# Splitting the prompt's q and k into high and low parts where they are projected, and scoring two attention heads in row tiles of TensorE

## The chip, the core and the metric

The kernel runs on one core of a Trainium2 chip. The core has five engines that run programs of their own and wait for each other on semaphores: TensorE (PE, matmuls, with its weight loads shown as PEld), VectorE (DVE), ScalarE (ACT), GpSimd (POOL) and SyncE (SP, which here only issues DMAs). The metric is the device time of one execution in microseconds (us); lower is better.

## The reference, cut to what matters

One step of a decoder layer for a prompt of 2048 tokens and 32 sample tokens (8 requests of 4), width 1024, all in float32. Half of the mixing width is a gated linear recurrence (HGRN), the other half is attention in 8 heads of 64 channels. Only the prompt's attention is touched by the change:

```python
proj = a @ w_in                                  # a = rmsnorm(x), q, k, v of attention are the last 3*512 columns
q_b = partial_rotary(qb, pos); k_b = partial_rotary(kb, pos)
for window, dil in ((128, 1), (512, 4), (2048, 16)):     # DILATIONS
    # positions of one residue mod dil form a sub-sequence; a query sees the last window/dil + 1 of its own
    s = where(valid, q*scale @ k, NEG_INF)               # blocks of 128 queries
    m = s.max(-1); p = exp(s - m); l = p.sum(-1); acc = p @ v
o_b = sum_d(exp(m_d - max m) * acc_d) / sum_d(exp(m_d - max m) * l_d)
h = x + concat(o_a, o_b) @ w_o;  h = h + ConvFFN(rmsnorm(h));  h = h + gate * (p @ w_ple_proj);  y = rmsnorm(h)
```

The kernel joins two of the dilations in one set of blocks with an additive mask, so the code has two kinds of blocks, `di` 0 and 1.

## The kernel before

The program has three parts in time. First **the projection** (`in_phase`, twice 1024 tokens, up to about 827 us): `x @ w_in` with each factor cut into a rounded high part and a low part, three matmuls for a product (L301, L302, L303). Its token groups go to q, k, v and so on; for a group of 128 prompt tokens `late()` turns q or k on TensorE (L324), copies it out of PSUM with one VectorE copy (L329, tile `oT`), and SP stores it to a scratch tensor in DRAM (L330, `qT_d`, `kT_d`). HGRN units run in the side. Then **the attention phase** (`attn_phase`, about 827 to 1208 us), and last the output projection, ConvFFN and embedding, two thirds of the time, which the change leaves alone.

In the attention phase the 8 heads are taken as 4 pairs `p`; a pair has 32 blocks of 128 queries: 16 with `di` 0 (the queries of one residue mod 4 in a chunk `c` of 512 tokens; it sees `nk` = c+1 groups of 128 keys) and 16 with `di` 1 (`nk` 2, the first one 1). For each block a pipeline of three steps runs over the turns of one loop:

- `scores`: matmuls into a PSUM tile S (one bank, two buffers), then for each head a VectorE reduction that adds the mask and takes the minimum (L724, into `st`) and a ScalarE exponential (L725). Signs are arranged so that the minimum serves as maximum. A block with `nk` 1 or 2 is one `Unit` for both heads; one with `nk` 3 or 4 is two `Unit`s, one a head.
- `turned`, two turns later: TensorE transposes P into a PSUM tile PT (L732), and one copy takes it to SBUF (L734, on ScalarE in every fourth turn, else on VectorE).
- `weighted`, three turns later: the product with v (L744) into `acc`, the two heads in the two column halves of TensorE; after four blocks ScalarE copies it out (L802).

Score precision: q is kept as high over low on 128 partitions (`qS`: 64 channels high, 64 low), k as `kH` and `kL`, both repeated on the two halves, so that two matmuls of K=128 make all four products. To build these, `stage` issues four SP DMAs for a chunk (L600, each half of the partitions twice), and `stack` runs on POOL two roundings (L142), two subtractions for the low half of q (L611) and two for `kL` (L616), on VectorE two casts into the residue order `q4` (L612), on ScalarE two casts `kH` (L615). There are 4 x 4 chunks.

`merge` joins the two kinds of blocks for a chunk: small VectorE and ScalarE work on the statistics, a store of coefficients to DRAM (L672), a load that spreads them over the partitions (L676, tile `cf`, two buffers), and two POOL multiplications (L681).

One turn in two, a step of the side work is put between: HGRN unit 7, then the sample tokens' attention (32 loads of 1 MB of cached keys and values, matmuls L844 and L880), then the samples' HGRN (L567, L570, L584). The framework's scheduler sets the final order on each engine by its own costs; each engine then runs its list in order.

## Time and profile before

| | |
|---|---|
| median of 3 runs | 3099.36 us (3092.71 to 3101.87) |
| the profiled execution | 3096.28 us, its span 3094.5 us |
| PE, DVE, ACT, POOL busy | 97%, 72%, 42%, 26% of the span |
| attention phase, 827 to 1208 us | 381 us, 12% of the span |
| PE, DVE, ACT, POOL busy in it | 339.5, 301.5, 241.0, 162.2 us |

A busy PE is not a PE at its peak: matmuls are pipelined and their ends are modelled, so that the distance between starts says what a matmul costs, and its own duration does not. Rows of groups give the line, the engine, the operation, the tiles, the count, the busy time and mean nanoseconds, and behind the bar the idle time of the engine ahead of it with what ended it. A row of the answer on windows gives, for a stretch, its length, then the busy time of PE, PEld, DVE, ACT and POOL (with counts), the granted clock of TensorE as a share of full speed, the share in which the 16 DMA engines were busy, and the GB/s they moved.

### The profile page before, as it was taken

What the parts mean: (1) busy time and instruction counts of PE and PEld (TensorE: products, weight loads), DVE (VectorE), ACT (ScalarE), POOL (GpSimd) and SP (SyncE); (2) the same over time, 40 slices, a digit from 0 to 9 for tenths busy, and PEclk for the clock granted to TensorE, in tenths of its full rate; (3) what the DMA queues carried; (4) which work ended last, traced back from release to release, by engine and by line L of the source; (5) the groups of instructions that cost most, each with busy time, mean ns of one, the idle gap of its engine ahead of it and who ended that gap; (6) DMA issues with size and microseconds to landing.
All of it is one profiled execution on the core that took longest, in us unless ns stands there. A gap on an engine that the chain in (4) does not pass through costs nothing.

```text
span 3094.5 us, 52057 instructions
## 1 busy us (share of the span) xinstructions
PE 2992.3 (97%) x19035; PEld 2785.2 (90%) x19035; DVE 2233.4 (72%) x4662; ACT 1295.2 (42%) x2813; POOL 806.6 (26%) x659
## 2 busy tenths in 40 slices
PE   9999999999889989999999999999999999999997
PEld 8988899987675667998999998999998999999997
DVE  7424667867587686568777779777789877777776
ACT  4111422222276564335444444444445444445443
POOL 1111122222343342002222232222222222222331
PEclk9999999999999999999999999999999999999998
DMA  5234333342539976673443445333434444436443
GB/s 185 93 121 135 105 104 104 106 141 81 158 79 284 285 225 218 237 265 139 137 133 113 133 156 168 124 126 131 144 119 162 153 139 139 144 116 219 132 166 130
DMA packets 265216, 467.97 MB, mean 151 GB/s; under 512 B 39360, under 2 KB 107072, under 8 KB 263168
## 3 DMA queue, kind: packets, MB, share of 16 engines
q1 hardware_dynamic: 261376, 397.66, 40.7%
q10 hardware_dynamic: 3584, 66.98, 6.1%
q8 instruction: 150, 2.46, 0.3%
q14 instruction: 106, 0.87, 0.1%
HBM read 381.05 MB, written 150.48 MB: 172 GB/s over the span
## 4 chain that ended last, share of the span: by engine, by line
PE 80%; DVE 12%; DMA 3%; issue 2%; ACT 1%; POOL 1%; SPq 0%; DVEq 0%; ACTq 0%; POOLq 0%
PE mm L136 18%; PE mm L137 18%; PE mm L138 18%; PE mm L301 3%; PE mm L302 3%; PE mm L303 3%; PE acc L744 1%; PE lv L441 1%; PE PT L732 1%; DVE w L910 1%; DVE P L724 1%; PE lv L301 1%; PE lv L303 1%; PE lv L302 1%; PE S L719 1%
## 5 line engine op out<-in xcount | busy, mean ns | idle before, releaser
L137 PE MATMUL mm<-w 128*128 128x352 f32 (+3 forms) x3768 | 1212.4, 322 | 4.3 <-DVE w L982 4.3
L138 PE MATMUL mm<-w 128*128 128x352 f32 (+3 forms) x3640 | 1164.0, 322 | 0.0
L136 PE MATMUL mm<-w 128*128 128x352 f32 (+3 forms) x3640 | 1138.7, 323 | 18.2 <-ACT w L981 8.7
L137 PEld LDWEIGHTS mm<-w 128*128 128x128 f32 x3768 | 712.9, 189 | 8.0 <-DVE w L982 7.8
L136 PEld LDWEIGHTS mm<-w 128*128 128x128 f32 x3640 | 681.8, 189 | 24.6 <-ACT w L981 10.6
L910 DVE TENSOR_TENSOR w<-raw,w 128x512 fp32r<-128x512 f32 x718 | 563.1, 799 | 179.5 <-ACT w L909 172.7
L138 PEld LDWEIGHTS mm<-w 128*128 128x128 f32 x3640 | 687.7, 189 | 0.1
L909 ACT CAST w<-raw 128x512 fp32r<-128x512 f32 x718 | 431.9, 620 | 396.3 <-PE mm L138 277.2
L1171 DVE TENSOR_TENSOR h<-h,mm 128x352 f32<-128x352 f32 (+1 forms) x528 | 257.6, 506 | 83.8 <-PE mm L138 83.2
L1103 POOL TENSOR_TENSOR raw<-raw 128x512 f32<-128x512 f32 x66 | 97.2, 1473 | 725.2 <-DMA raw<-in_w_gate_dram 251.0
L1111 POOL TENSOR_TENSOR raw<-raw 128x512 f32<-128x512 f32 x66 | 93.4, 1414 | 384.8 <-DVE w L910 384.8
L725 ACT ACTIVATE P<-P,st 128x256 f32<-128x256 f32 (+3 forms) x256 | 134.3, 527 | 75.5 <-DVE st L724 68.4
L1126 ACT COPY s<-mm 128x352 f32<-128x352 f32 (+1 forms) x198 | 88.2, 445 | 173.7 <-PE mm L138 169.2
L301 PE MATMUL mm<-wh,xh 128*128 128x512 f32 x352 | 142.0, 405 | 0.0
L303 PE MATMUL mm<-wh,xl 128*128 128x512 f32 x352 | 140.9, 401 | 0.0
L302 PE MATMUL mm<-wl,xh 128*128 128x512 f32 x352 | 140.4, 400 | 0.0
L142 POOL TENSOR_SCALAR wh<-wraw 128x512 fp32r<-128x512 f32 x96 | 72.0, 762 | 245.5 <-PE o L137 82.5
L136 PE MATMUL mm<-xh,wh 128*128 128x384 f32 (+2 forms) x384 | 124.9, 330 | 5.6 <-ACT xh L199 4.9
L724 DVE CUSTOM_DVE_ANT_0 P<-S,mask 128x256 f32<-128x256 f32 (+3 forms) x256 | 105.6, 445 | 29.7 <-PE S L720 25.3
L963 POOL TENSOR_TENSOR w<-w 128x704 f32<-128x704 f32 (+2 forms) x42 | 75.1, 1794 | 198.9 <-ACT w L962 198.2
L224 DVE TENSOR_TENSOR wl<-wraw,wh 128x512 fp32r<-128x512 f32 x104 | 84.6, 835 | 58.2 <-POOL wh L142 52.1
L138 PE MATMUL mm<-xh,wl 128*128 128x384 f32 (+2 forms) x384 | 125.1, 329 | 1.3 <-DVE wl L224 1.2
(337 smaller groups left out, 5156.3 us busy)
## 6 DMA issues: line engine op xcount, KB each, us to landing
raw<-in_w_gate_dram SPq DMA_DIRECT2D x132, 256.0 KB
raw<-in_w_up_dram SPq DMA_DIRECT2D x132, 256.0 KB
raw<-in_w_down_dram SPq DMA_DIRECT2D x132, 256.0 KB
out_sk_dram<-in_cache_k_dram ACTq DMA_DIRECT2D x56, 584.0 KB
out_sv_dram<-in_cache_v_dram ACTq DMA_DIRECT2D x56, 584.0 KB
wraw<-in_w_in_dram SPq DMA_DIRECT2D x104, 256.0 KB
raw<-in_w_ple_gate_dram SPq DMA_DIRECT2D x64, 256.0 KB
raw<-in_w_o_dram SPq DMA_DIRECT2D x48, 256.0 KB
```

What stands on the lines that cost most here:

```text
L136: PE.matmul(ps, lhsT=wh, rhs=xh, start=first, stop=False, skip_group_check=read)
L137: PE.matmul(ps, lhsT=wh, rhs=xl, start=False, stop=False, skip_group_check=read)
L138: PE.matmul(ps, lhsT=wl, rhs=xh, start=False, stop=last, skip_group_check=read)
L301: PE.matmul(ps, lhsT=xh[k][:, js], rhs=wh, start=k == 0, stop=False)
L302: PE.matmul(ps, lhsT=xh[k][:, js], rhs=wl, start=False, stop=False)
L303: PE.matmul(ps, lhsT=xl[k][:, js], rhs=wh, start=False, stop=k == NK - 1)
L724: V.tensor_tensor_reduce(pe, s[:, w * i:w * i + w], bl.mask, 1.0, 3e38, ALU.add, ALU.min, mn)
L725: A.activation(pe, pe, AF.Exp, bias=mn, scale=-1.0, accum_out=st[:, bl.r, hh, 0:1])
L909: A.copy(w[:, 0], raw)
L910: V.tensor_sub(w[:, 1], raw, f32(w[:, 0]))
L1103: G.tensor_add(s1, a21, a22)
L1171: V.tensor_add(h[m][:, cs], h[m][:, cs], ps[:, :H])
```

## The change

`late()` now makes both parts itself: a ScalarE copy rounds the turned q or k to the high part (for k in the residue order within 128 tokens), a VectorE subtraction makes the low part, and SP stores both; 64 stores in all where there were 32. The scratch tensors have a dimension for high and low. In the attention phase `fetch` loads a chunk of q and of k, both parts at once, with two DMAs on POOL's own queue (a software queue, which the kernel did not use so far), and `stack` is left with two POOL roundings that put q into `q4`. Gone are the SP loads of `stage`, the subtractions L611 and L616 and the casts L612 and L615.

A score is three products, high by high, high by low, low by high, each of K=64; the two heads of a pair sit in the upper and lower 64 partitions and go to the two row tiles of TensorE, so three pairs of matmuls stand where two heads had two matmuls each. S is one tile of two banks (`S = pS.tile([128, 2, 512])`, made once), one for each head; blocks with one or two key groups use its halves in turn. A block is one `Unit` for both heads; where `nk` is 3 or 4 it has two PT tiles, one copied by VectorE and one by ScalarE, and takes two turns of the side work. Lines of the second kernel are a few higher: scores L727, transposes L743, products L753, `cf` multiplications L683, roundings L144, loads L618.

```diff
@@ in_phase, late()
-                            oT = ev.tile([128, 4, 128], F32, name="oT", bufs=2)
-                            V.tensor_copy(oT, ptv)
-                            SP.dma_start((qT_d if kind == "q" else kT_d)[:, :, tok:tok + 128], oT)
+                            oT = [ev.tile([128, 4, 128], F32R, name="oT", bufs=3) for _ in range(2)]
+                            hi, lo, pv = *oT, ptv
+                            if kind == "k":
+                                hi, lo = [t.rearrange("p a (r i) -> p a r i", r=4) for t in (hi, lo)]
+                                pv = ptv.rearrange("p a (i r) -> p a r i", r=4)
+                            A.copy(hi, pv)
+                            V.tensor_sub(lo, pv, f32(hi))
+                            for i in range(2):
+                                SP.dma_start(f32((qT_d if kind == "q" else kT_d)[:, i, :, tok:tok + 128]), f32(oT[i]))
@@ attn_phase
...
+        def fetch(p, c):
+            cs = slice(512 * c, 512 * c + 512)
+            for i, (t, src) in enumerate(((q, qT_d), (k, kT_d))):
+                if p or c:
+                    G.dma_start(t[:, :, cs], src[:, :, p, cs])
+                else:
+                    A.copy(t[:, 0, cs], first[i][:, 0])
+                    round_g(t[:, 1, cs], first[i][:, 1])
+        def stack(c):
+            for x in range(2):
+                round_g(q4[:, x, :, 128 * c:128 * c + 128],
+                        f32(q[:, x, 512 * c:512 * c + 512]).rearrange("p (i r) -> p r i", r=4))
@@ Unit.scores
-                s = pS.tile([128, 512], F32, name="S")
-                for i, hh in enumerate(self.heads):
-                    PE.matmul(s[:, w * i:w * i + w], lhsT=bl.q(hh), rhs=bl.k(kH, hh), start=True, stop=False)
-                    PE.matmul(s[:, w * i:w * i + w], lhsT=bl.q(hh), rhs=bl.k(kL, hh), start=False, stop=True)
+                s = S[:, :, self.at:self.at + w]
+                for i, (a, b) in enumerate(((0, 0), (0, 1), (1, 0))):
+                    for hh in range(2):
+                        PE.matmul(s[:, hh], lhsT=bl.q(hh, a), rhs=bl.k(hh, b), start=i == 0, stop=i == 2,
+                                  tile_position=(64 * hh, 0))
@@ Unit.turned
-                (A.copy if on_act else V.tensor_copy)(out[:, :n], pt[:, :n])
+                for i, heads in enumerate(((0,), (1,)) if nk > 2 else ((0, 1),)):
...
+                    act = i if nk > 2 else on_act
+                    (A.copy if act else V.tensor_copy)(self.pt[:, heads[0]:heads[-1] + 1], pv)
@@ when chunks are loaded and prepared, in blocks ahead of their use
-                    x = begin[p, 0, 0] - 10 + 4 * c
-                    at(x - 7, lambda p=p, c=c: staged.append(stage(p, c)))
-                    at(x, lambda p=p, c=c: stack(c, *staged.pop(0)))
+                        x = begin[p, 0, 0] - 6 + 4 * c
+                    at(x - 6, lambda p=p, c=c: fetch(p, c))
+                    at(x - 2, lambda c=c: stack(c))
```

**TensorE, two blocks of `di` 1.** In the rows below S is the score tile, PT the transposed P, acc the product with v, and 128x256 is the size written. Before, a block of two heads:

```order
L719 MATMUL S<-kH,qS 128x256 [waits DVE_49]
L720 MATMUL S<-kL,qS 128x256
L719 MATMUL S<-kH,qS 128x256
L720 MATMUL S<-kL,qS 128x256
L732 MATMUL PT<-c_ident,P 128x128 [waits DVE_49,Activation_49]
L732 MATMUL PT<-c_ident,P 128x128 [waits Activation_49]
L744 MATMUL acc<-pt,v 64x128
L744 MATMUL acc<-pt,v 64x128 [waits Activation_49]
L744 MATMUL acc<-pt,v 64x128 x6
```

And in the changed kernel, such a block (p 3):

```order
L727 MATMUL S<-k,q 128x256 [waits DVE_49]
L727 MATMUL S<-k,q 128x256 x5
L743 MATMUL PT<-c_ident,P 128x128 [waits Activation_49]
L743 MATMUL PT<-c_ident,P 128x128
L743 MATMUL PT<-c_ident,P 128x128 [waits Activation_49]
L743 MATMUL PT<-c_ident,P 128x128
L753 MATMUL acc<-pt,v 64x128 [waits DVE_49]
L753 MATMUL acc<-pt,v 64x128 x3
```

Four matmuls became six. The wait on VectorE ahead of the first of them was, before, for the minimum of the S tile two back (in 145 of 166 cases); now it is for that of the block right ahead (126 of 127), since both halves belong to one tile S. The side work stands earlier against the blocks: HGRN unit 7 ended near block 34 and now near block 16, the samples' attention ran over blocks 40 to 106 and now 21 to 76, the samples' HGRN over 113 to 127 and now 79 to 94.

**POOL at the start of the attention phase.** ssq and rb are the two tiles in which the first chunk was loaded. Before:

```order
L142 TENSOR_SCALAR qS<-ssq 128x512 [waits PE_49]
L142 TENSOR_SCALAR qS<-ssq 128x512
L611 TENSOR_TENSOR qS<-ssq,qS 64x512 [waits Pool_49]
L616 TENSOR_TENSOR kL<-rb,kH 128x4x128 [waits PE_49,Activation_49,Pool_49]
L611 TENSOR_TENSOR qS<-ssq,qS 64x512 [waits Pool_49]
L616 TENSOR_TENSOR kL<-rb,kH 128x4x128 [waits Activation_49,Pool_49]
L142 TENSOR_SCALAR qS<-stage 128x512 [waits DMAHW7_49,DMAHW0_49]
L142 TENSOR_SCALAR qS<-stage 128x512
```

Now (q_8221 is `q4`; the waits of the second load are for stores into `kT_d`):

```order
L144 TENSOR_SCALAR q<-ssq 128x512 [waits PE_49]
L144 TENSOR_SCALAR k<-rb 128x512
L618 DMA k<-kT_d 128x2x512
L618 DMA k<-kT_d 128x2x512 [waits DMAHW3_49,DMAHW5_49,DMAHW2_49,DMAHW7_49,DMAHW1_49,DMAHW0_49]
L144 TENSOR_SCALAR q_8221<-q 128x4x128 [waits PE_49,Pool_49]
L144 TENSOR_SCALAR q_8221<-q 128x4x128 [waits Activation_49]
L618 DMA q<-qT_d 128x2x512 [waits Pool_49]
```

The six POOL operations that made the first chunk are four, with two loads between them.

**POOL between the first and the second pair of heads.** o_ are the accumulated outputs. Before:

```order
L616 TENSOR_TENSOR kL<-stage,kH 128x4x128 [waits DMAHW6_49,DMAHW5_49,Activation_49]
L616 TENSOR_TENSOR kL<-stage,kH 128x4x128 [waits Activation_49]
L611 TENSOR_TENSOR qS<-stage,qS 64x512 [waits Pool_49]
L611 TENSOR_TENSOR qS<-stage,qS 64x512
L681 TENSOR_TENSOR o_8398<-o_8398,cf 128x512 [waits DMAHW5_49,DMAHW4_49,Pool_49]
L681 TENSOR_TENSOR o_9168<-o_9168,cf 128x512
L826 MEMSET qb 128x1024 [waits DVE_49]
L681 TENSOR_TENSOR o_8570<-o_8570,cf 128x512 [waits DMAHW6_49,DMAHW5_49]
L681 TENSOR_TENSOR o_9305<-o_9305,cf 128x512
```

Now:

```order
L683 TENSOR_TENSOR o_8464<-o_8464,cf 128x512 [waits DMAHW1_49,DMAHW0_49]
L683 TENSOR_TENSOR o_9212<-o_9212,cf 128x512 [waits DMAHW2_49,Activation_49]
L144 TENSOR_SCALAR q_8221<-q 128x4x128 [waits DMASW4_49]
L144 TENSOR_SCALAR q_8221<-q 128x4x128
L618 DMA q<-qT_d 128x2x512 [waits Pool_49]
L683 TENSOR_TENSOR o_8683<-o_8683,cf 128x512 [waits DMAHW2_49,DMAHW1_49]
L683 TENSOR_TENSOR o_9341<-o_9341,cf 128x512 [waits DMAHW3_49,Activation_49]
L683 TENSOR_TENSOR o_8920<-o_8920,cf 128x512 [waits DMAHW7_49,DMAHW0_49]
L683 TENSOR_TENSOR o_9473<-o_9473,cf 128x512 [waits Activation_49]
L144 TENSOR_SCALAR q_8221<-q 128x4x128 [waits DMASW5_49]
L144 TENSOR_SCALAR q_8221<-q 128x4x128
```

Before, the work on the second pair's q and k was over ahead of the first multiplication by `cf`; now the roundings of its chunks 2 and 3 stand behind the multiplications of the first pair's chunks 0, 1 and 2. Blocks 40 and 44 are the first to need them.

103 lines of the change are left out of this document (44 added, 59 removed).

## The prediction

> **What bounds the kernel now.** I read the windows first, to see how much of the span the change can reach. The columns are the stretch, its length, the busy time of PE, PEld, DVE, ACT and POOL, the clock granted to TensorE, the share in which the DMA engines were busy, and GB/s.
>
> ```profile
> 100.00:400.00 300.00, 300.00 (x1527) 253.97 (x1526) 126.49 (x325) 63.89 (x126) 39.67 (x56) 1.00 0.36 115
> 827.30:859.00 31.70, 21.68 (x119) 17.71 (x117) 29.40 (x84) 19.23 (x49) 24.67 (x23) 0.73 0.68 173
> 859.00:886.20 27.20, 26.90 (x237) 22.09 (x234) 22.67 (x67) 17.29 (x42) 0.00 (x0) 1.00 0.18 40
> 1014.30:1067.70 53.40, 47.29 (x391) 30.24 (x389) 32.70 (x106) 28.73 (x83) 16.66 (x14) 0.97 1.00 272
> 1110.80:1208.00 97.20, 90.25 (x819) 64.67 (x815) 77.74 (x281) 58.10 (x182) 34.65 (x33) 0.96 0.71 205
> 827.00:1208.00 381.00, 339.50 (x2889) 241.16 (x2888) 301.46 (x985) 241.00 (x698) 162.24 (x141) 0.94 0.76 217
> ```
>
> The attention phase, the last row, is 381 us, an eighth of the span. TensorE is busy for 339.5 of it, so even perfect cover would save 41.5 us, 1.3% of the kernel; anything beyond needs less work on TensorE itself. The idle time isn't spread evenly. The first eight blocks (827.3 to 859) have 10 us of it: VectorE is busy 29.4 of 31.7 us there and sets the pace, and TensorE ran at 0.73 of its clock. The next eight (859 to 886.2) are bound by TensorE. In the middle the DMA engines are full (1.00 in the fourth row). The end (1110.8 to 1208) has 7 us of idle.
>
> Then I asked for the waits of TensorE in this phase (total us, times, longest):
>
> ```profile
> PE S L719 <- DVE st L724: 11.9, 12, 2.5
> PE acc L744 <- DVE pt L734: 8.7, 9, 1.8
> PE s L441 <- DVE at L453: 6.0, 4, 4.1
> PE PT L732 <- DVE pt L734: 4.2, 6, 1.9
> PE s L584 <- DVE hso L582: 2.5, 1, 2.5
> ```
>
> All five wait for VectorE. So the change's lever is VectorE's list in this phase, and its danger is the first row: the score matmul that waits until the minimum has read its S tile.
>
> **The change, part by part.** The groups of the attention phase that it touches, and, last, the one copy in the projection:
>
> ```profile
> L612 DVE CAST q<-qS 128x512 fp32r<-128x512 f32 x31 | 25.1, 810 | 0.0
> L734 DVE COPY pt<-PT 128x512 f32<-128x512 f32 (+2 forms) x120 | 74.2, 621 | 31.5 <-PE PT L732 27.5 <-PE acc L744 3.6
> L615 ACT CAST kH<-stage 128x512 fp32r<-128x512 f32 x30 | 32.8, 1141 | 7.7 <-DMA stage<-kT_d 4.0 <-PE S L719 3.1 <-issue 0.5
> L724 DVE CUSTOM_DVE_ANT_0 P<-S,mask 128x256 f32<-128x256 f32 (+3 forms) x256 | 105.6, 445 | 29.7 <-PE S L720 25.3 <-PE S L719 1.6 <-ACT pt L734 1.2
> L329 DVE COPY oT<-ms 128x512 f32<-128x512 f32 x32 | 21.9, 687 | 20.6 <-PE ms L324 20.0 <-DMA qT_d<-oT 0.5
> ```
>
> *Projection.* 32 VectorE copies of 0.69 us become 32 subtractions; between 0.69 and the 0.81 us of a cast in residue order that is 0 to 4 us more for VectorE. 32 ScalarE copies of up to 1.14 us (L615) add 37 us, and 32 more stores SP's issue time. I cost all of it at nothing: the first window, in the projection, has TensorE busy for all 300 us with VectorE at 42%, ScalarE at 21% and the DMA engines at 36%. Without that cover it would be at most the 37 us; what isn't covered is the last group, whose turn ends at the phase's start (below).
>
> *First chunk.* What POOL did ahead of the first block, and the first score matmul:
>
> ```profile
> 820.02 1.20 POOL L142 TENSOR_SCALAR qS<-ssq 128x512 fp32r<-128x512 f32 x2 [48.96 <-PE mm L302]
> 821.30 1.36 POOL L611 TENSOR_TENSOR qS<-ssq,qS 64x512 fp32r<-64x512 f32 x1
> 822.74 1.52 POOL L616 TENSOR_TENSOR kL<-rb,kH 128x512 fp32r<-128x512 f32 x1
> ...
> 825.68 1.81 POOL L616 TENSOR_TENSOR kL<-rb,kH 128x512 fp32r<-128x512 f32 x1
> 827.37 0.36 PE L719 MATMUL S<-kH,q 128*128 128x128 f32 x1
> ```
>
> Two subtractions of each kind and two roundings kept POOL from 820.02 to 827.5. Now it is four roundings (4 x 0.6 = 2.4 us) and two DMA issues. No issue on POOL's software queue is in the trace: as little as nothing, or, as an upper end, 1.8 us like POOL's longest step here. I take 0.75 us, near to what SP spends on one (2.92 us for four, below). That is 3.9 us, so about 3 us earlier, unless the second load's wait for the stores of `kT_d` holds the queue; it can eat these 3 us, and no more than about 3 beyond.
>
> *Casts off VectorE.* 32 casts of 0.81 us go. Five of them (4.7 us) lie between 827.3 and 859:
>
> ```profile
> L612 DVE CAST q<-qS 128x512 fp32r<-128x512 f32 x5 | 4.7, 934 | 0.0
> ```
>
> There VectorE is the bound, so they count in full, and a TensorE that idles less should be granted more than 0.73; I add 1 us for that. The start gives -3 - 5 - 1 = **-9 us** (between 0 and -14). Next in line there is the recurrence's own work on VectorE, which now stands against 17 blocks rather than 35 and takes some of it back; this is why I don't take more.
>
> The other 20 us of casts, and 16 PT copies of 0.62 us that go from VectorE to ScalarE (the wide blocks now alternate: VectorE has 104 of the copies, not 120), relieve it by 30 us where TensorE isn't waiting for it most of the time. The waits that this can shorten are those for `pt`, 8.7 + 4.2 us, less these, which lie ahead of 860:
>
> ```profile
> PE acc L744 <- DVE pt L734: 3.2, 2, 1.8
> ```
>
> I take half: **-5 us** (between 0 and -10). ScalarE loses 33 us of casts and gains 9 us of copies; POOL loses its subtractions, and neither bounds anything here.
>
> *Passes on TensorE.* Starts say what a matmul costs, so here are rows in order of time, with N=256 (scores) and N=128 (transposes, products), and from the projection N=512:
>
> ```profile
> 1070.10 0.29 PE L719 MATMUL S<-kH,qS 128*128 128x256 f32 x1
> 1070.22 0.28 PE L720 MATMUL S<-kL,qS 128*128 128x256 f32 x1
> 1070.34 0.60 PE L732 MATMUL PT<-c_ident,P 128*128 128x128 f32 x4
> 1070.87 0.43 PE L744 MATMUL acc<-pt,v 128*64 128x128 f32 x2
> ```
> ```profile
> 818.61 0.40 PE L301 MATMUL mm<-wh,xh 128*128 128x512 f32 x1
> 818.84 0.39 PE L302 MATMUL mm<-wl,xh 128*128 128x512 f32 x1
> ```
>
> From start to start, N=256 costs 0.12 us and N=512 0.23. Four transposes of N=128 last 0.60, one 0.27 (the three pitches between are 0.11). N=384 I put midway at 0.18. The 128 blocks have 20, 76, 16 and 16 of the four widths. Four full passes a block are 4 x (20 x 0.11 + 76 x 0.12 + 16 x 0.18 + 16 x 0.23) = 72 us. If the two row tiles run side by side, three passes are 54, that is -18. No pair of row tiles is in the trace. The nearest are the column pairs of L744, of which this run
>
> ```profile
> 953.29 0.87 PE L744 MATMUL acc<-pt,v 128*64 128x128 f32 x10
> ```
>
> has ten in 0.87 us where two take 0.43 (above): four more pairs in 0.44, 0.11 a pair, so a pair costs as much as one. I take three passes.
>
> Against that stand changes of the tile shape. Four transposes should let the next start after 0.44 us; the L744 behind them, in another shape, starts 0.53 after. So a change costs 0.09. In the order of the phase's matmuls there are 367 changes before and 565 after, since each group of scores is now a shape of its own: 198 x 0.09 = +18. Passes and changes together: **0 us**, between -18 (free changes) and, with six loads in a row at 0.11 to 0.23 (108 us for 72, were nothing side by side), +54.
>
> [...]
>
> ```profile
> L570 PEld LDWEIGHTS s<-hsvm,hskt 32*128 32x128 f32 x64 | 7.7, 186 | 1.3 <-issue 0.6 <-POOL o L681 0.2
> L720 PEld LDWEIGHTS S<-kL,qS 128*128 128x128 f32 x128 | 24.9, 195 | 1.5 <-issue 1.4
> ```
>
> [...] No run here shows row tiles.
>
> *One S tile.* The reduction of a block with `nk` 2 took, with its start 0.42 us after the start of the block's last matmul (1072.69 by the trace of TensorE):
>
> ```profile
> 1072.69 0.28 PE L720 MATMUL S<-kL,qS 128*128 128x256 f32 x1
> ```
> ```profile
> 1073.11 0.42 DVE L724 CUSTOM_DVE_ANT_0 P<-S,mask 128x256 f32<-128x256 f32 x1 [1.08 <-PE S L720]
> ...
> 1073.81 0.08 DVE L724 DVE_READ_ACCUMULATOR2_ANT st<- 128x1 f32 x1
> ```
>
> With the next block's scores held until the minimum is out, a turn is at least 0.24 (to the third pass) + 0.42 + 0.78 + about 0.1 for the semaphore = 1.54 us. TensorE's own work in such a turn is 0.36 for scores, 0.44 for four transposes, 0.22 for two pairs of products and three changes of shape, 1.3 us. So a turn with no side work waits 0.25 us; queued behind the scores are the transposes and products of two older blocks, which the wait delays too. With a step of side work in it, a turn waits for nothing. By the built order the bare turns are about 39, 33 of them at the end: **+10 us** there, less the 7 us of idle that stand there now and of which the waits for S are the larger part. I take +6 on balance (from -4 to +32, all 128 turns paying). The last wait (L584, 2.5 us) goes, as the samples' recurrence ends 30 blocks earlier: **-2.5 us**.
>
> *POOL's queue.* The roundings of the second pair's chunk 3 now stand behind the `cf` multiplications:
>
> ```profile
> 954.80 2.92 SPq L676 DMA_DIRECT2D cf<-coef_d  x4
> ```
> ```profile
> 967.34 5.44 POOL L681 TENSOR_TENSOR o<-o,cf 128x512 f32<-128x512 f32 x4 [32.68 <-DMA cf<-coef_d]
> ```
>
> A `cf` load lands some 10 us after its issue there, in a stretch with full DMA engines, and what is queued behind the waiting POOL is now a block's q. From the load's place in the order to the block that needs the chunk are four blocks, at 3 us each 12 us. Just in time, or late by up to 8; the same for the third pair. I take +2 and +1 = **+3 us** (0 to +16).
>
> The sum: -9 - 5 + 0 + 6 - 2.5 + 3 = -7.5 on the profiled 3096.3 us (span 3094.5, 1.8 around it), which gives 3088.8. The median of the runs shown, 3099.4, lies 3.1 above that execution, so against it the same is 3091.9. The forecast is between the two, **3090**. About 0.3% of 3099, 9.3 us, is what a measurement of this kernel can tell from no change.
>
> **The rivals.**
>
> *The loads of the two row tiles queue* (slower). Six loads, 0.11 us behind each other (the pitch of the narrowest matmuls), with the moving data side by side: 128 x 6 x 0.11 = 84.5 instead of 54, +30 on TensorE. Against it the column pairs, for it that they share rows and not columns. About a third of it falls in turns that wait anyway: 3090 + 20 = 3110. It decides once a pair costs over 0.165 us: three passes of 128 blocks are 384 pairs, 0.14 each in the sum, and 0.025 more on each is the whole gain of 9.
>
> *The one S tile decides everywhere* (slower or the same). 11.9 us of waits at twelve turns with two buffers show that VectorE is sometimes late; with one, each of its bursts (merges, the recurrence) holds the next scores. All 128 turns at 0.25 us are 32 instead of 10: 3090 + 22 = 3112; half of that is no change or little more.
>
> *POOL late at several places* (slower or the same): 8 us at blocks 44 and 76 and again at the start, 3090 + 13 to 17, about 3105.
>
> *VectorE's relief carries through* (faster): all waits for `pt` gone (another -5), the bare turns as fast as now (-6) and the start by -14 (another -5), 3074, or with most of the changes of shape free down to 3060.
>
> *No change that can be seen.* In the middle the DMA engines are full (1.00), the sample loads of 32 MB now stand within 55 blocks rather than 66, and TensorE would wait for them instead of VectorE. What is won at the start is given back there: 3096.
>
> **Chances.** Forecast (3079 to 3099) 0.42, of which 0.25 is faster by over 0.3% and 0.17 within; relief carries through 0.13, faster; queueing loads 0.15, slower; one S tile 0.14, 0.08 slower and 0.06 the same; POOL 0.08, 0.05 slower and 0.03 the same; DMA-bound 0.08, 0.06 the same and 0.02 faster. In sum 0.40 faster, 0.32 the same, 0.28 slower. The range is 3062 to 3116: it leaves out the upper half of the queueing and one-tile cases and the last of the gains, 2 in 10. The likeliest case's own is 3079 to 3099.
>
> **What would show it.** The phase should last about 373 us. Two score matmuls of a pair should start within some 10 ns and the next pair 0.11 to 0.12 us later; six starts 0.11 apart are the first rival. Between 827 and 859 VectorE should be below 90% and TensorE's clock above 0.73. In the last 33 blocks, waits of the scores for `st` of 0.2 to 0.3 us at nearly every turn; the same all over the phase is the second rival. A wait of block 40, 44, 72 or 76 for POOL is the third. Waits for the sample loads above the present few us are the last. I am wrong outright if the projection's end moves, or if waits of the kind S behind `st` add up to more than 30 us.

## The result, and the profile after

The changed kernel takes **3122.07 us** (median of 7 runs, 3108.97 to 3128.63) where the kernel before takes 3099.36. The ratio is 1.0069, with a 95% interval of [1.0049, 1.0090]: slower by 0.7%. The forecast was 3090 with a range of 3062 to 3116, so it was wrong in sign, and the time lies outside the range. The profiled execution took 3124.57 us, its span 3122.8, which is 28.3 longer than the span before.

First the stretches of the changed kernel, in the columns of the prediction (length, busy time of PE, PEld, DVE, ACT, POOL, granted clock, DMA share, GB/s): the first eight blocks, the next eight, the stretch from the middle of the last pair to the end, the whole attention phase, and all behind it.

```profile
830.00:862.00 32.00, 26.45 (x194) 20.28 (x194) 26.36 (x95) 15.80 (x49) 11.26 (x12) 0.84 0.51 138
862.00:890.00 28.00, 28.00 (x248) 20.59 (x248) 19.28 (x63) 19.55 (x61) 0.95 (x1) 1.00 0.06 17
1110.00:1234.00 124.00, 114.18 (x927) 77.23 (x926) 84.05 (x314) 71.24 (x228) 37.37 (x36) 0.83 0.54 153
830.00:1234.00 404.00, 368.17 (x3138) 234.78 (x3138) 255.55 (x939) 218.46 (x682) 105.45 (x105) 0.90 0.69 204
1234.00:3122.00 1888.00, 1839.86 (x11521) 1827.16 (x11521) 1434.54 (x2313) 844.70 (x1619) 488.33 (x320) 0.98 0.44 152
```

and the last row's counterpart in the kernel before:

```profile
1208.00:3094.00 1886.00, 1838.82 (x11522) 1825.97 (x11522) 1436.31 (x2322) 844.59 (x1619) 485.24 (x319) 0.98 0.46 152
```

The part behind the phase is 2 us longer; the phase itself is 404 instead of 381. VectorE did get lighter (255.6 us busy, 301.5 before), and so did POOL (105, 162). But TensorE, whose work the forecast took as unchanged in sum, is busy for 368 us instead of 339.5, and its clock fell from 0.94 to 0.90. In this view 0.06 x 381 = 23 us went to the lowered clock before, and 0.10 x 404 = 40 now.

The waits of TensorE in the phase (total us, times, longest), the largest rows and those that the prediction names:

```profile
PE S L727 <- DVE st L732: 9.0, 11, 2.2
PE PT L743 <- ACT P L733: 3.3, 3, 2.4
PE s L853 <- DMA skt<-in_kT_d_dram: 3.1, 1, 3.1
PE s L853 <- DMA skt<-in_kT_w_dram: 2.9, 3, 2.2
PE s L449 <- DVE at L461: 2.8, 2, 2.5
PE s L889 <- DMA skt<-in_v_w_dram: 2.4, 1, 2.4
PE acc L753 <- DVE pt L745: 2.3, 3, 1.5
```

The score's wait for the minimum is shorter than before (9.0, before 11.9), that of the products for `pt` fell from 8.7 to 2.3, and three rows with 8.4 us are loads of the samples' cached keys and values. All waits for such loads come to 9.5 us, where they were 2.0 before.

To part work from waits and clock I took the distances between the starts of all matmuls of the phase, left idle time out, and weighted each with the clock granted in its 2-us window. At full clock that is, in us:

| | scores | transposes | products | side work | sum | idle |
|---|---|---|---|---|---|---|
| before | 93.1 | 72.5 | 86.7 | 68.1 | 320.4 | 41.1 |
| after | 77.5 | 91.2 | 89.2 | 71.8 | 329.7 | 35.2 |

So in the profiled pair, of +28.3 us, about 3 lie ahead of the first score (827.4, now 830.3), 23 in the phase and 2 behind it. The 23 are +9 of work, -6 of idle time, and +19 of clock (lost in the phase: 22.4 us before, 41.2 after, from windows of 4 us).

This split counts a microsecond at half clock as half a microsecond of work, which is too little. In the changed kernel at a granted clock of 0.50:

```profile
1122.39 1.01 PE L727 MATMUL S<-k,q 64*128 64x256 f32 x6
1123.33 1.12 PE L743 MATMUL PT<-c_ident,P 128*128 128x128 f32 x4
1124.37 1.12 PE L753 MATMUL acc<-pt,v 128*64 128x128 f32 x8
1125.42 0.66 PE L575 MATMUL s<-hs,hsEb 128*32 128x128 f32 x8
```

From start to start six scores take 0.94 us, four transposes 1.04 and eight products 1.05; at full clock the same groups take 0.56, 0.59 and 0.58 (rows further down). That is 1.7 to 1.8 times as long and not twice, so about a seventh of what is counted as clock lost in such stretches is really work: by this estimate the profiled 23 us are some 12 of work, -6 of idle time and 16 of clock.

A single execution doesn't settle the clock: it varies from run to run (0.978 to 0.985 over the whole span before, 0.973 to 0.983 in the changed kernel). For every run the mean granted clock is known, so "clock lost" below is (1 - mean clock) x span. Over all runs of the kernel before (85) it is 59.4 us on the mean, over those of the changed kernel (13) 70.3. Of a mean difference of 20.8 us in time, **10.9 is clock and 10.0 is the rest**, which is about the work, the start and the part behind the phase, less the idle time. With the seventh taken off it is rather 9 and 11.5. The profiled execution was one that lost much.

### The profile page after: what moved, and what is told of

It is laid out like the page before. It is cut to its first block, busy times and chain, and to the rows that moved or that the text cites. A ratio compares the mean times of both kernels' runs of the same rounds, so it can differ in the third digit from the quotient of the medians.

```text
span 3122.8 us, 52542 instructions
## 1 busy us (share of the span) xinstructions
PE 3024.7 (97%) x19291; PEld 2780.7 (89%) x19291; DVE 2187.3 (70%) x4614; ACT 1290.0 (41%) x2831; POOL 754.6 (24%) x627
## 4 chain that ended last, share of the span: by engine, by line
PE 52%; DVE 5%; issue 1%; ACT 1%; DMA 1%; POOL 0%; DVEq 0%; SPq 0%; ACTq 0%; POOLq 0%
PE mm L138 17%; PE mm L139 17%; PE mm L140 17%; DVE w L919 1%; DVE h L1180 1%; PE mm L125 0%; DVE w L991 0%; DVE w L1296 0%; ACT w L990 0%; DVE w L1254 0%; DMA w<-in_pT_dram 0%; DVE w L1265 0%; PE mm L110 0%; DVE w L1353 0%; DVE w L1093 0%
## 5 line engine op out<-in xcount | busy, mean ns | idle before, releaser
L144 POOL TENSOR_SCALAR wh<-wraw 128x512 fp32r<-128x512 f32 x96 | 73.7, 779 | 246.6 <-PE o L139 81.4
L139 PE MATMUL mm<-xl,wh 128*128 128x384 f32 (+2 forms) x384 | 124.4, 327 | 0.6 <-DVE xl L202 0.6
```

The source lines that it names most:

```text
L139: PE.matmul(ps, lhsT=wh, rhs=xl, start=False, stop=False, skip_group_check=read)
```

## The experiments

| kernel | median us | ratio [95%] | clock lost, mean us | span less that |
|---|---|---|---|---|
| before (85 runs) | 3098.5 to 3102.8 in seven groups | 1 | 59.4 | 3039.1 |
| changed, again | 3122.46 | 1.0074 [1.0058, 1.0089] | 70.7 | 3050.2 |
| full_array | 3148.58 | 1.0159 [1.0142, 1.0176] | 88.1 | 3059.2 |
| four_passes | 3143.61 | 1.0135 [1.0120, 1.0150] | 73.1 | 3069.1 |
| sp_loads | 3113.29 | 1.0047 [1.0032, 1.0061] | 68.5 | 3043.1 |
| sp_loads_2 | 3114.28 | 1.0041 [1.0025, 1.0057] | 66.4 | 3046.8 |
| hs_k128 | 3117.85 | 1.0059 [1.0043, 1.0075] | 63.4 | 3053.1 |
| hs_late | 3117.04 | 1.0051 [1.0039, 1.0063] | 67.3 | 3047.5 |
| side_late | 3117.54 | 1.0056 [1.0036, 1.0075] | 64.6 | 3053.0 |
| side_late_sp | 3120.74 | 1.0055 [1.0034, 1.0077] | 69.7 | 3048.8 |
| before_short | 3095.17 | 0.9974 [0.9963, 0.9986] | 56.8 | 3036.5 |
| pt_twice | 3128.84 | 1.0095 [1.0072, 1.0117] | 61.5 | 3065.8 |
| dense_fill | 3112.94 | 1.0050 [1.0032, 1.0069] | 54.5 | 3057.8 |
| before_fill | 3103.75 | 1.0015 [1.0006, 1.0025] | 57.0 | 3045.4 |
| sp_fill | 3122.07 | 1.0073 [1.0060, 1.0086] | 60.9 | 3059.7 |
| products_full | 3076.74 | 0.9938 [0.9922, 0.9954] | 58.5 | 3018.8 |
| before_shapes | 3126.95 | 1.0100 [1.0083, 1.0117] | 60.7 | 3065.2 |
| before_same | 3113.11 | 1.0047 [1.0035, 1.0060] | 52.4 | 3058.5 |

The clock lost scatters by 4 to 9 us over the runs of one kernel; with 5 or 6 runs its mean is uncertain by some 3 us.

### The changed kernel again

> The changed kernel once more, for a second profile of it. Theory A (clock): TensorE's work at full clock is what it was, and the time is lost because the granted clock stays at half for long after short waits. Lost clock, counted as (1 - granted clock) x time from the first score to the end of the phase, was 22.5 us before and 41.5 us after. A expects the lost clock to be other in this profile, with the stretches at half elsewhere or of another length, and the time to go with it: the phase's length less the lost clock should again be about 362 us. Theory B (work): the six row-tiled matmuls and the 198 more changes of tile shape cost TensorE more than they save, some 20 us; then the phase less its lost clock is longer than that of before (358 us) by 15 us or more in every profile. Theory C (side work): the sample tokens' work, now 20 to 35 blocks earlier, brings waits for loads; then waits of L853, L889 and L575 for DMAs add up to 15 us or more.

3122.46 us: the result stands. In its profile the phase takes 395 us, 32 of it clock, so 363 are left, as theory A has it and not the 373 or more of theory B. Waits of L853, L889 and L575 for loads come to 8.7 us, not C's 15. But the time did not follow the phase's clock as A expects, since 6 us more than in the first profile were lost to the clock behind the phase. Of the 27 us over the span before, 4 lie ahead of the phase, 15 in it and 8 behind it. And the stretches at half clock are elsewhere: 27 us at the start of the phase (from 827) and 10 at 1124, where the first profile had 34 from 1117. So where such a stretch stands is a matter of the execution, and a single profile of a variant can't tell that it removed one.

### Are the row tiles themselves slow?

They aren't. This is the answer in order of time, in the changed kernel, for a piece of the last pair of heads; the third row is six score matmuls.

```profile
1179.22 0.66 PE L743 MATMUL PT<-c_ident,P 128*128 128x128 f32 x4
1179.81 0.66 PE L753 MATMUL acc<-pt,v 128*64 128x128 f32 x8
1180.39 0.62 PE L727 MATMUL S<-k,q 64*128 64x256 f32 x6
1180.95 0.66 PE L753 MATMUL acc<-pt,v 128*64 128x128 f32 x8
```

Six of N=256 last 0.62 us, the next shape starts 0.56 after them: three passes of 0.12 and a change, and not six. That refutes the rival of queueing loads. Nor is a single weight load shorter for its half height (median 186 ns at 64 rows, L727; 188 to 190 at 128 rows in the kernel before, L719): all six, and their matmuls, fit into the 0.56 us. The same rows show what the prediction mis-sized: four transposes, at 0.11 apart, let the next shape start after 0.59, not 0.44; four pairs of products after 0.58; the scores' change costs 0.56 - 0.36. That is 0.14 to 0.20 us a change of shape where 0.09 was put. The kernel before had the fuller price in view too, where a change stood on both sides of four transposes:

```profile
894.26 1.09 PE L744 MATMUL acc<-pt,v 128*64 128x128 f32 x14
895.27 0.66 PE L732 MATMUL PT<-c_ident,P 128*128 128x128 f32 x4
895.86 0.44 PE L744 MATMUL acc<-pt,v 128*64 128x128 f32 x4
```

Here they take 0.59 from start to start, as in the changed kernel. The four transposes that the prediction read, 0.53, stood right behind scores of their own shape: only the change behind them was in the reading, the 0.06 us of the one ahead was not.

**full_array** undoes the row tiles: q high over low on 128 partitions, k on both halves, two matmuls of K=128 for each head.

```diff
-                    for hh in range(2):
-                        PE.matmul(s[:, hh], lhsT=bl.q(hh, a), rhs=bl.k(hh, b), ..., tile_position=(64 * hh, 0))
...
+                for hh in range(2):
+                    for x in range(2):
+                        PE.matmul(s[:, hh], lhsT=bl.q(hh), rhs=bl.k(hh, x), start=x == 0, stop=x == 1)
```

> Row tiles alone undone: the split at the projection, the loads on POOL's queue, the one S tile of two banks and one unit a block stay; q's high part lies over its low part and k's parts are repeated on both halves, so that a head's scores are two matmuls of K=128 as before (four DMAs more for a chunk and 0.5 MB more). A: 387 changes of shape in place of 565 and matmuls that use the whole array let the clock recover in 4 to 8 us after each wait; lost clock 25 us or less, time 3085 to 3100. B: 3095 to 3105, with the lost clock still near 40. C: the side work stays earlier than before by 10 to 25 blocks, so 3110 to 3120.

26 us more than the changed kernel, and more than any of the three theories asked for. TensorE's work at full clock fell to 323.3 (387 changes of shape instead of 565), but idle time rose from 35 to 51: waits for the samples' cached keys and values come to 17.1 us, waits of the scores for the minimum to 15.1. A chunk now takes six POOL-issued loads, not two, which may be why; no run parts it. The clock lost rose to 88, so the clock is lowered without row tiles as well. A wait of 3.5 us for a load here stood in this stretch at half clock, near its start:

```profile
PE s L575 <- DMA hs<-in_state_dram: 3.5, 1, 3.5
```
```profile
1155.00:1197.00 42.00, 38.48 (x207) 27.47 (x206) 19.24 (x75) 12.97 (x47) 20.08 (x24) 0.52 0.82 205
```

**four_passes** adds the fourth product (low by low) as a fourth pair, so that as many columns stream as before.

```diff
-                for i, (a, b) in enumerate(((0, 0), (0, 1), (1, 0))):
+                for i, (a, b) in enumerate(((0, 0), (0, 1), (1, 0), (1, 1))):
```

> The changed kernel with the fourth product, low by low, as a fourth pair of row-tiled matmuls in each block: 128 more pairs of 0.11 to 0.23 us, 18 us of TensorE at full clock, with the same changes of shape (a more exact result, no other change). Theory A in its strong form (the third of the columns that the change took out of each score group is what lets the half clock hold): lost clock 55 to 62 and time 3124 to 3134, less than the 18 us added. If the share of columns isn't what counts: lost clock 68 or more, time 3136 to 3144.

21 us slower; the clock lost did not fall (73). So fewer streamed columns alone are not the reason either. It also prices a pair pass: work rose by 353.4 - 329.7 = 24 us for 128 of them, 0.19 each over widths of 128 to 512.

### What do the loads on POOL's queue cost?

**sp_loads** issues them on SP, nothing else.

```diff
-                    G.dma_start(t[:, :, cs], src[:, :, p, cs])
+                    SP.dma_start(f32(t[:, :, cs]), f32(src[:, :, p, cs]))
```

> The loads of q and k go over SP's queue and not over POOL's software queue; everything else as in the changed kernel. Theory A: the lost clock and the time stay, 3116 to 3126. Rival (POOL's software queue delays the chunks or the sample loads): 5 us or more faster, under 3115. Theory C (DMA engines full): no change, since the same bytes move.

> The loads on SP's queue once more, since with the superfluous matmuls added their gain was not seen. If the gain of 9 us is a property of this program: 3110 to 3116 again, span less lost clock 3043. If it was the runs: 3118 to 3124.

3113.29 and, measured a second time, 3114.28: 8 to 9 us of the loss go when the loads leave POOL's queue for SP's, 2 to 6 of them outside the clock. In the changed kernel POOL did this at the start:

```profile
820.38 0.62 POOL L144 TENSOR_SCALAR q<-ssq 128x512 fp32r<-128x512 f32 x1 [49.24 <-PE mm L304]
820.96 0.62 POOL L144 TENSOR_SCALAR k<-rb 128x512 fp32r<-128x512 f32 x1
821.52 1.67 POOL L618 DMA_DIRECT2D k<-kT_d  x2
823.22 2.23 POOL L144 TENSOR_SCALAR q<-q 128x512 fp32r<-128x512 f32 x2
825.41 0.76 POOL L618 DMA_DIRECT2D q<-qT_d  x1
```

These two issues took 0.83 us each (the median of all 30 is 0.72 for k, 0.76 for q), near the 0.75 taken; the roundings into residue order took 1.1 us each, not 0.6. So POOL needed 5.1 us for the first chunk where 3.9 was put. It was still done before its old time, but the first score then waited for something new, VectorE's subtraction for the last k group:

```profile
830.32 0.90 PE L727 MATMUL S<-k,q 64*128 64x128 f32 x6 [0.99 <-DVE oT L336]
```
```profile
825.27 0.58 ACT L335 CAST oT<-ms 128x512 fp32r<-128x512 f32 x1 [2.52 <-PE ms L326]
...
825.58 0.68 DVE L426 TENSOR_TENSOR at<-s,c_ident 128x512 f32<-128x512 f32 x1
...
829.48 0.69 DVE L336 TENSOR_TENSOR oT<-ms,oT 128x512 fp32r<-128x512 f32 x1
```

ScalarE had the high part ready at 825.85. VectorE came to the subtraction 3.6 us later, because work of the recurrence (L426, L461, L388) stood ahead of it in its list.

Without the issues the first score comes at 829.0 instead of 830.3, and idle time in the phase is 32.5 and 31.2 us instead of 35.2. That is 4 to 5 us of the 8. Where the rest comes from is open.

### Does the clock depend on where the samples' work stands?

This is what happened to the clock in the changed kernel. Two short waits:

```profile
1114.68 1.12 PE L578 MATMUL s<-hsvm,hskt 32*128 32x128 f32 x8 [0.78 <-DVE hsn L581]
1116.21 0.43 PE L575 MATMUL s<-hs,hsEb 128*32 128x128 f32 x8 [0.41 <-DMA hs<-in_state_dram]
```

and what followed, by windows; the last row is the whole stretch:

```profile
1115.00:1120.00 5.00, 4.59 (x35) 2.99 (x34) 2.99 (x13) 2.16 (x8) 1.43 (x2) 0.66 0.78 214
1120.00:1125.00 5.00, 5.00 (x32) 3.84 (x34) 3.61 (x14) 0.68 (x2) 1.94 (x3) 0.50 0.68 182
...
1117.00:1150.00 33.00, 33.00 (x196) 22.75 (x196) 21.07 (x81) 10.37 (x37) 11.30 (x13) 0.50 0.73 205
```

For 33 us TensorE is busy without a gap and still has half its clock: 16 us lost as the clock counts, some 14 by the lengths of the groups. In the kernel before, at the like place and after a wait of 1.9 us, it has it back in the next window:

```profile
1115.00:1120.00 5.00, 4.94 (x30) 2.81 (x31) 4.25 (x19) 1.85 (x9) 2.12 (x2) 0.66 0.30 91
1120.00:1125.00 5.00, 5.00 (x49) 3.34 (x48) 3.22 (x16) 3.15 (x14) 0.00 (x0) 1.00 0.98 316
```

In the record of the clock the half lasts 3.4 us there and 34.1 us in the changed kernel. So back-to-back issue didn't bring the clock back by itself in that stretch, and the shorter waits (0.78 and 0.41 us, against 1.9) have the longer one behind them.

**hs_k128** gives the samples' recurrence matmuls (L578, K=32) 128 rows, the added ones zero.

```diff
-            vm = hp.tile([NS, 512], F32, name="hsvm", bufs=2)
-            G.tensor_scalar(vm, va_s, bmask[:, bb:bb + 1], 1.0, ...)
+            vm = vms[bb % 2]                      # [128, 512], zeroed once
+            G.tensor_scalar(vm[:NS], va_s, bmask[:, bb:bb + 1], 1.0, ...)
```

> Only the samples' HGRN changes: its state updates (K=32, a row tile of 32) become K=128 with 96 rows of zeros, in the same place and number. [...] B and C: 3118 to 3126, no change.

3117.85, just under the 3118 to 3126 of B and C; clock lost 63.4, between the 59.4 of before and the 70.3 of the changed kernel. Its profile has no long stretch near 1117 (14 us at 1153), but the changed kernel's own second profile has none there either: inconclusive.

**hs_late** holds the samples' recurrence back to blocks 110 to 124 by a tiny VectorE copy that needs a later block's statistics.

```diff
+        V.tensor_copy(F[0:1, 0:1], latest[0])       # latest: a block's minimum
...
+        V.tensor_copy(qb[0:1, 0, 0, 0:1], latest[0])     # the same ahead of the samples' attention
...
-        if turn % 2:
+        if turn % 8 in (1, 4, 6):
```

> The changed kernel with the samples' HGRN put back to the end of the phase (blocks 110 to 124, where it stood at 113 to 127 before; 79 to 94 in the changed kernel), by a tiny VectorE copy that its first step waits for and a slower pace of the side work; nothing else moves. Over all runs so far the lost clock, (1 - mean granted clock) x span, is 58 us before and 71 us in the changed kernel, and the span less the lost clock 3040 and 3050. Theory A (clock, lost where the samples' HGRN runs beside narrow blocks of 256 keys): lost clock 58 to 63, time 3108 to 3114. Theory B (TensorE's own work: shape changes): no change of either, 3118 to 3126. Theory C (sample loads earlier, waits for DMAs that let the clock drop): no change either, since the loads stay early.

67 us lost, where theory A asked for 58 to 63, and a stretch at half clock is there, now with no side work in it and behind a wait of 2.3 us:

```profile
1118.00:1146.00 28.00, 26.22 (x154) 16.14 (x154) 16.14 (x63) 14.44 (x53) 10.12 (x9) 0.53 0.53 150
```

**side_late** also spreads the samples' attention over blocks 25 to 106, by such a copy ahead of each of its 32 loads; **side_late_sp** does both and loads q and k on SP.

```diff
+                    V.tensor_copy(kt[0:1, 0, 0:1], latest[0])
...
+                    V.tensor_copy(vt[0:1, 0, 0:1], latest[0])
```

> As the one before, and the samples' attention spread too (blocks 25 to 106; 40 to 104 before, 21 to 76 in the changed kernel), by a tiny VectorE copy ahead of each of its 32 loads. A: as the one before, 3108 to 3114. C: waits for the loads in the phase fall from 9.5 us to under 4, lost clock 55 to 60, time 3100 to 3108. B: the span less the lost clock stays at 3050 or rises by the 32 copies, so that even with the lost clock of before the time is 3108 or more.

> The changed kernel with the side work spread as in side_late and the loads on SP's queue, the two changes that each undo one thing the trace shows as worse than before. If the position of the side work is worth 5 us of lost clock and the loads 5 us of the rest: lost clock 62 to 66, span less lost clock 3044 to 3048, time 3106 to 3112. If the waits for sample loads, 24 us with spread loads, come from POOL's software queue, they fall under 10 us and the time is 3100 to 3106.

Neither brought the time back (3117.5, 3120.7). Late loads make new waits, 24 us in all, of which the largest

```profile
PE s L896 <- DMA skt<-in_v_w_dram: 6.9, 2, 4.0
```

so that the place of the side work can't be called innocent by this run; the runs only show that moving it back doesn't bring the clock back.

**before_short** is the mirror: in the kernel before, the samples' products with v in their second half are cut from N=512 to 64, most of these outputs left out.

```diff
-                        PE.matmul(acc[rows], lhsT=PT[:, 4 * si + i, rows], rhs=vt[:, bi], ...)
+                        nv = 64 if g and si + i else 512
+                        PE.matmul(acc[rows, :nv], lhsT=PT[:, 4 * si + i, rows], rhs=vt[:, bi, :nv], ...)
```

> The mirror of the superfluous matmuls, on the kernel before: in the second half of the samples' attention (requests 4 to 7, which stands beside blocks 86 to 106) the products with v from the second load on are cut from N=512 to N=64 (28 matmuls; most of those outputs are left out), with the same loads, order and changes of shape. TensorE has about 1.5 us less to do. Theory A (long matmuls beside the narrow blocks are what brings the clock back after a wait): lost clock 65 to 75 in place of 59, time 3102 to 3112. Rival (the lost clock of the changed kernel has nothing to do with the long matmuls that it moved away): lost clock 56 to 62, time 3095 to 3101.

4 us less work and no rise of the clock lost (56.8, where theory A asked for 65 to 75): that the long columns of this side work hold the clock up in the kernel before is refuted.

### Do longer runs of one shape bring the clock back?

**pt_twice** does each transpose of blocks 72 to 103 twice.

```diff
-                    for hh in heads:
+                    for hh in heads * (2 if 72 <= self.x < 104 else 1):
```

> Every transpose of P in blocks 72 to 103 is issued twice, some 135 more full-array matmuls of N=128 at 0.11 us, 15 us of work that changes nothing in the result. A, if dense full-array work lifts the clock: lost clock falls by 10 us or more and the time hardly rises, 3115 to 3125. B and C: the work is simply added, 3132 to 3140.

Its time rose by only 7 us, between what A and B asked for: the span less the clock lost rose by 17, while 9 us less were lost. More work of the plain full-array shape raised the clock.

**dense_fill** puts two superfluous full-array matmuls of N=512 ahead of the transposes in 18 turns, **before_fill** the same in 18 turns of the kernel before, **sp_fill** the same on top of sp_loads.

```diff
+                    for _ in range(2 if 86 <= self.x < 104 else 0):
+                        PE.matmul(pt, lhsT=q[:, 0, :128], rhs=k[:, 0, :512], start=True, stop=True)
```

> The changed kernel with two superfluous full-array matmuls of N=512 ahead of the transposes in each of blocks 86 to 103 (they write the PT tile that the transposes then overwrite): 36 x 0.23 = 8 us more for TensorE at full clock, and no result changes. In these blocks the clock stayed at half for 10 to 34 us in the profiles so far, with TensorE issuing without a gap but streaming columns in only 0.13 to 0.28 of the time that a full clock would allow; where it came back to full, the share was 0.28 to 0.30 or more. Theory A (the half clock holds itself up because short matmuls between changes of shape stream too little): the long matmuls lift the share over that, lost clock 55 to 62 (70 in the changed kernel), time 3112 to 3120, in spite of the added work. Theories B and C: the 8 us are added, 3126 to 3134, lost clock 70 or more.

> Control on the kernel before: the same two superfluous matmuls of N=512 ahead of the transposes of blocks 86 to 103, 36 x 0.23 = 8 us of work. There the clock is at half only for some 4 us in these blocks. Theory A: nothing to win, so the time rises by 4 to 9 us, 3104 to 3109, and the lost clock stays within 5 us of 59. Rival (dense work lifts the clock everywhere, or the gain of the same work in the changed kernel came from another order): lost clock falls by 8 us or more and the time stays or falls, 3100 or less.

> The changed kernel with both helps: loads on SP's queue and the superfluous matmuls in blocks 86 to 103. If the two gains (9 us each alone) are of different causes, 3101 to 3107, lost clock 50 to 58 and span less lost clock 3048 to 3053; if the loads' gain was lost clock too, 3110 to 3114.

With 36 superfluous matmuls added the changed kernel became **9 us faster**, because the clock lost fell from 70 to 54.5. The phase of its profile, beside 0.90 in the changed kernel:

```profile
831.00:1220.00 389.00, 357.93 (x3174) 227.47 (x3174) 251.87 (x937) 218.56 (x682) 105.58 (x105) 0.96 0.70 211
```

In the kernel before, the same work costs 4 us and moves the clock little (57.0): there was no such stretch to fill. With the loads on SP, though, the fill made things worse (3122): the clock lost fell from 67 to 61, but the rest rose by 13 to 17 us, more than the 8 put in. The profiles part this: the matmuls raise TensorE's work by 13 to 14 us in both (by the measure of the table of work, some of it owed to the half clock), but idle time in the phase falls from 35 to 31 us in dense_fill, and rises to 35.5 in sp_fill from 31.2 and 32.5 with the loads on SP alone. So the two gains don't add up; why the idle time goes the other way stays open.

### Do the changes of shape cost the time?

The built order of the phase has 367 changes of tile shape before and 565 now. Theory A has them keep the clock down as well as cost time of their own; in theory B the clock falls with waits and stays down whatever the shapes.

**products_full** takes changes out of the changed kernel: one product with v over the full array (both heads' channels as 128 columns, the first head's P) where a pair of column halves stood. The second head's product is left out, so its time is that of an incomplete kernel.

```diff
-                    for hh in range(2):
-                        PE.matmul(acc[hs, bl.r], lhsT=vals[bl.p, bl.di, c][:, r, hs], rhs=self.pt[:, hh, i], ...,
-                                  tile_position=(0, 64 * hh))
+                    PE.matmul(acc[:, bl.r], lhsT=vals[bl.p, bl.di, c][:, r], rhs=self.pt[:, 0, i], ...)
```

> The changed kernel, in which the product with v is one matmul of the full array (both heads' channels as its 128 columns, with the first head's P) where a pair of column halves stood; the second head's product is left out. By the built order, changes of tile shape in the attention phase go from 565 to 357, below the 367 of the kernel before; the count of passes stays. Work alone: 208 changes at 0.09 to 0.17 us are 19 to 35 us less on TensorE, of which the idle time takes perhaps half. Theory A (frequent changes of shape keep the clock at one half): the clock lost, averaged over the runs, falls from 70 us to 56 to 60, so that the time is some 22 to 35 us below the changed kernel's, 3087 to 3100. Theory B (the clock falls with waits and stays down whatever the shapes): 65 to 73 us lost, and the time falls by the work alone, 3100 to 3112.

**before_shapes** puts about as many into the kernel before, by a 16-column matmul of half height ahead of each group of transposes; **before_same** is its control with full height.

```diff
+                PE.matmul(pt[:, 0, :16], lhsT=qS[0:64, 0, 0:128], rhs=kH[0:64, 0, 0, 0:16], ...)   # before_shapes
+                PE.matmul(pt[:, 0, :16], lhsT=qS[:, 0, 0:128], rhs=kH[:, 0, 0, 0:16], ...)         # before_same
```

> The kernel before, with one superfluous matmul of 16 columns and half height (K=64) ahead of each group of transposes (160 of them): changes of tile shape in the attention phase go from 367 to 588, a little over the changed kernel's 565. Its work is 221 changes at 0.09 to 0.17 and 160 pitches of some 0.06, 30 to 48 us, of which idle time takes some 15 to 20. Theory A: the clock lost rises from 58 us towards 70 in the mean of the runs, with stretches of 10 us and more at half clock behind a wait, so some 6 to 12 us more on top; 3120 to 3140. Theory B: the clock lost stays at 56 to 60, as in the control with matmuls of the full height; 3112 to 3125.

> Control: the kernel before, with the same 160 superfluous matmuls of 16 columns, but of full height (K=128), in the shape of the transposes behind them: 399 changes of shape where 367 stood. Both theories: 10 to 18 us of work, partly in idle time, +3 to +12, 3103 to 3112, and 56 to 60 us of lost clock. What the half-height version takes beyond this is what changes of shape cost.

In order of time, first of before_shapes, then of before_same:

```profile
1073.01 0.27 PE L731 MATMUL PT<-kH,qS 64*128 64x16 f32 x1
1073.21 0.55 PE L733 MATMUL PT<-c_ident,P 128*128 128x128 f32 x3
```
```profile
1074.34 0.28 PE L731 MATMUL PT<-kH,qS 128*128 128x16 f32 x1
1074.47 0.66 PE L733 MATMUL PT<-c_ident,P 128*128 128x128 f32 x4
```

The same 16 columns take 0.20 us when a change of shape follows and 0.13 when none does. Over the phase, TensorE's work is 358.8 us in the one and 345.0 in the other: 13.8 for 588 - 399 = 189 changes, **0.07 us each**. In time they differ by 13.8 us as well (3126.95, 3113.11), but by another sum: 8 us of it are clock, and idle time, 36 us in the one profile and 28 in the other, took up 9 us of the work. In products_full the work fell from 329.7 to 299.6, 30 us for 208 changes, **0.145 each**, if one full product costs what a pair of halves did. By the distances between starts it does where the number of pairs is even (four full products 0.447 us, 0.112 each), but an odd number of pairs takes as long as one pair more (two products 0.363, four 0.370). The changed kernel has 50 such groups, some 5 us that this run saves too, so the price is 0.12 to 0.145. The time fell by 45 us, below the kernel before.

On the clock the two theories both fail in part. Lost clock goes the way of theory A both times: 70 to 58.5 with fewer changes, 52.4 to 60.7 with more, each by some 2.5 times its uncertainty. But before_same itself lost less than expected (56 to 60) and less than the kernel before (59.4), which before_shapes only comes back to. And it stays far below the 70 that A asked for; its phase has no long stretch at half clock but for one of 24 us at its start:

```profile
825.00:1228.00 403.00, 375.36 (x3044) 268.38 (x3045) 301.63 (x990) 241.23 (x697) 162.14 (x141) 0.95 0.72 202
```

and products_full, with fewer changes than the kernel before, has one in its profiled execution:

```profile
1110.00:1138.00 28.00, 27.33 (x149) 20.26 (x149) 17.86 (x75) 10.86 (x41) 8.40 (x10) 0.50 0.88 255
```

So the changes of shape may weigh on the clock, but they aren't the condition that keeps it down. **That condition stays open.** Excluded by runs, as a needed condition or as the sole cause, are the row tiles, the number of streamed columns, the place of the samples' recurrence and the changes of shape; long full-array matmuls in blocks 86 to 103 lower the loss from 70 us to 54.5.

One regularity of the profiles narrows it down, found afterwards and tested by no run. In the record of the clock it changes only at steps of 3.41 us: in the phase of the two kernels' profiles every stretch at half clock is a whole number of them, from 3.4 to 34.1 us. Between 840 and 1190 us the 19 profiles have 172 such steps at half clock in which TensorE never waits. Count for each step the columns that its matmuls stream, each matmul by the share of the 128x128 array that its operands fill. The clock came back at the end of 41 of 48 steps with 2000 columns or more, of 59 of 99 with 1400 to 2000, and of 1 of 25 below 1400. All 25 of those are in the changed form and its variants, and eight of the ten steps of the 33-us stretch have less than 1900. A superfluous full-array matmul of N=512 puts 512 columns into this sum, and a change of shape, at 0.07 to 0.2 us, leaves less of the step for columns. It isn't the whole condition: 7 steps over 2000 stayed at half, and four_passes raises the sum of its scores without a lower mean loss.

No complete version that was run beats the kernel before; the best of the new form is the one with its loads on SP, 0.4 to 0.5% slower.

## Why the prediction was wrong

Against its own sum of -7.5 us, the profiled executions differ by +28.3, the means of the runs by +20.8. Term by term:

- **Projection, 0: right.** POOL's first rounding, which waits for its end, comes at 820.38, before at 820.02.
- **Passes, -18: right.** The scores' own time fell by 15.6 us, with one change of shape more in each group, and the row tiles run side by side (six matmuls of N=256 in 0.56 us, a change included).
- **Changes of shape, +18: the step that failed for the work.** Transposes, products and side work rose by 18.7, 2.5 and 3.7 us, 25 for the 198 added changes, 0.13 each; by single rows it is 0.14 to 0.20, by products_full 0.12 to 0.145. The price of 0.09 was read from one group of transposes that had a change behind it and none ahead of it. Passes and changes are together +9 (+12 with the work that the half clock hides), not 0.
- **Clock, -1: the second step that failed, for half of the loss.** The granted clock was asked only at the start, where it did rise (0.73, now 0.84; in the second profile it was at half until 855), and taken as given for the rest of the phase, where it fell: +19 in the profiled pair, +11 in the mean (16 and 9 with the seventh taken off). The sign would have been wrong without it, since the rest is +10 by itself. Nothing of it was in the range, nor in any rival; the +54 at its upper end stood for something else, the loads' queueing.
- **Start, -9: about -0.6.** The ninth block starts at 859.0, before at 859.6. VectorE's casts went as said (it is busy 82% there, before 93%), but the first score came 3 us later rather than 3 earlier. POOL's chain took 5.1 us, not 3.9, still less than the 7.5 before. Next in line was the subtraction for the last group of k, a step that the change itself puts on VectorE, and it stood behind the recurrence's work there. The text named both, but it costed the subtraction at nothing but for the last group, and then did not cost the last group.
- **Relief of VectorE, -5: right in kind.** The waits for VectorE's `pt` fell from 12.9 to 3.0 us, with ScalarE's from 14.8 to 4.2.
- **One S tile, +6: wrong.** Waits of the scores for the minimum fell by 2.9 us, and from 1155 us on, where one of 0.25 us was to stand at nearly every turn, there are three, 3.4 us in all. TensorE's own turn is longer than the 1.3 us of the text: the scores of blocks 108 to 111 start 1.72 to 2.25 us apart without waiting, more than the 1.54 that the chain over the minimum needs. (No run shows the 0.1 for the semaphore in that sum: scores that wait start 0.055 us after the end of the minimum.) The rival built on it is refuted.
- **Last wait, -2.5:** gone. In its place stand waits for the samples' loads, 9.5 us where there were 2.0, which the rival of full DMA engines named.
- **POOL's queue, +3:** no score matmul waited for POOL in the changed kernel (once in its second profile, 0.3 us). But the loads on POOL's queue do cost 8 to 9 us in all against SP's, in two runs, where only 0.75 us an issue at the start and late chunks were put.

Without the two failed steps the account is close, idle time fell by 6 us, but this is partly luck: the start was off by 8 us one way and the S tile by 9 the other. The forecast took TensorE's own time as known because TensorE was to do fewer passes, and looked for all risk in the waits.

## What to carry to other kernels

Count the changes of tile shape on TensorE before splitting a full-array product into tiles: here each costs 0.07 to 0.2 us, as much as a whole matmul of N=128 (0.11) or 256 (0.12). Price them from groups with a change on both sides, and from several of them. When a change shortens matmuls in a stretch that TensorE bounds, read the granted clock there by windows of a few us, before and after, in more than one run: a kernel that waits less can still run slower (here 35 us of idle time instead of 41, in a phase of 404 instead of 381). And before moving loads to POOL's software queue, run both: here SP's queue was 8 to 9 us better, though not once the superfluous matmuls were in.

## What was not expected of the hardware

- After waits of 0.4 to 0.8 us TensorE can stay at a granted clock of 0.50 for 33 us while it is busy 33.00 of 33.00 us; in another kernel it was back within 5, and in a second execution of the same one such a stretch stood elsewhere.
- At a granted clock of 0.50, groups of matmuls with a change of shape on both sides took 1.7 to 1.8 times as long as at 1.00, not twice.
- 36 superfluous matmuls of N=512 made a kernel 9 us faster (3122 to 3113).
- The products in the two column halves come in twos of pairs: one pair took 0.363 us from start to start between changes of shape, two pairs 0.370.
- A change of shape between neighbours costs 0.07 us (16-column matmuls, half against full height) to 0.2 (behind scores in row tiles).
- A DMA issue on POOL's software queue took 0.72 to 0.83 us, and a rounding of 128x512 that reorders its elements 1.1 us where the plain one took 0.6.
